# A SwiGLU / state-space / dilated-attention layer: gate output transposes as 32x32 blocks on the vector engine, and three smaller edits

## The chip, the cores and the metric

One core of one Trainium2 chip runs the whole layer. The core has five engines with a queue each: TensorE (PE in the profile, its weight loads apart as PEld), VectorE (DVE), ScalarE (ACT), GpSimd (POOL) and SyncE (SP), which here only starts DMAs. The metric is device time in microseconds of one execution, the median of several. Differences below about 0.2% can't be told from none.

## What is computed

The layer is a gated feed-forward block, a mixer (a state-space group and a dilated attention group side by side), and a second feed-forward block, each with a root-mean-square norm ahead of it; everything is float32, 256 tokens, model width 2048, hidden width 5504.

```python
def swiglu(x, w_gate, w_up, w_down):
    return (jax.nn.silu(x @ w_gate) * (x @ w_up)) @ w_down

h = h + 0.5 * swiglu(rmsnorm(h, ffn1_norm), ffn1_w_gate, ffn1_w_up, ffn1_w_down)
hn = rmsnorm(h, mix_norm)
...            # projection to q, k, v, u; s5_mixer; dilated_attention
h = h + mixed @ w_out
h = h + 0.5 * swiglu(rmsnorm(h, ffn2_norm), ffn2_w_gate, ffn2_w_up, ffn2_w_down)
return rmsnorm(h, final_norm)
```

## The kernel before

**Products in three parts.** Every large product is made of pairs of float32r halves. A weight piece of 4 x 128 rows and up to 512 columns is loaded by SP into one of three `wraw` buffers (`wraw`, L75). For two of its 128-row blocks at a time, `halves` writes the high half on ACT (L88, `whi`) and the low half on DVE (L89, `wlo`); each has four buffers. Such a pair of blocks is called a step here. `mm3` (L94 to L96) then issues three matmuls for each block and each of the two blocks of 128 tokens: high by high, high by low, low by high. A step is thus 12 matmuls. `product` (L98) walks over the steps, and between them pops work from two queues: `soon` (transposes of what has just been made) and `later` (steps of the mixer's preparation or of its scans, by `step`).

**The feed-forward block.** `ffn` (L266) goes over 11 chunks of hidden columns, ten of 512 and a last one of 384. For each it makes a gate product `G` and an up product `U` (eight steps each), then for each token block ACT writes `silu(G)` (L282) and DVE multiplies it with `U` (L283) into a tile `silu`. Its transposition is appended to `soon`: `transpose_split` (L136) makes one TensorE transpose for each 128x128 block into PSUM (L142), then ACT and DVE write the halves `xh` and `xl` of the result (L146, L147). It is popped after the second step of the next product. A full chunk has eight such transposes, the last chunk six. After the chunks, four down products `Y` over all 43 blocks use these halves, and `last_chunk` or `finish_chunk` squares the result for the next norm.

**Start and end.** `setup` issues 12 matmuls on zeros (L203) while the first pieces are loaded. In the very first gate product the input comes transposed from HBM, is split by `split_x` (L237, L238), and its first weight piece is loaded and split in three parts of 1, 1 and 2 blocks. At the end, `ffn2` issues 24 matmuls on zeros (`probe`) beside the last norm, which runs on ACT, DVE and POOL and ends with eight DMAs of the output.

**What sets the order.** Each engine works through its own queue in order. A scheduler sets that order when the program is built, by priorities and an assumed duration of each instruction, under the dependencies; buffers are reused only when the last reader is done. During the first feed-forward block the mixer's preparation (`prepare`) stands in `later` and is worked off a piece a step; it is used up ahead of the last five chunks. In the second block `later` is empty.

Of the kernel before, what the change touches and what calls it, by code (L numbers as in the profile page):

```python
# [31 lines left out]
class Layer:  # L32
# [4 lines left out]
    def __init__(self, ctx, tc, ins, out):  # L37
        self.tc, self.nc, self.t, self.out = tc, tc.nc, ins, out
        pool = lambda name, bufs, **kw: ctx.enter_context(tc.tile_pool(name=name, bufs=bufs, **kw))
        self.const = pool("const", 1)  # L40
        self.wpool = pool("weights", 2)
        self.slots = pool("slots", NSLOT)
        self.work = pool("work", 2)
        self.psum = pool("psum", 1, space=PSUM)
        self.dram = pool("scratch", 1, space=DRAM)
        self.n = 0
        self.later = deque()
        self.soon = deque()
        self.fetch = None

# [30 lines left out]

    def halves(self, raw):

        nc = self.nc
        _, nk, n = raw.shape
        hi = self.wpool.tile([P, 2, 512], F32R, tag="whi", bufs=4, name=self.name("whi"))
        lo = self.wpool.tile([P, 2, 512], F32R, tag="wlo", bufs=4, name=self.name("wlo"))
        nc.scalar.activation(hi[:, :nk, :n], raw, AF.Copy)  # L88
        nc.vector.tensor_sub(lo[:, :nk, :n], raw, hi[:, :nk, :n].bitcast(F32))  # L89
        return hi, lo  # L90
# [6 lines left out]

    def product(self, accs, xT, w, r0, nkt, c0, n, tail=0):  # L98


        held = []
        for k0 in range(0, nkt, 4):
# [3 lines left out]
            if self.fetch is not None:  # L106
                self.fetch(k0 // 4 + 1)
            xh, xl = xT[k0 // 4]
            for kk, ke in ((0, 1), (1, 2), (2, 4)) if opening else ((0, 2), (2, 4)):
# [3 lines left out]
                if self.fetch is not None:  # L113
                    self.split_x(k0 + kk, k0 + ke)
                wh, wl = self.halves(raw[:, kk:ke, :n])
                for k in range(kk, ke):
# [10 lines left out]
                while self.soon and k0 + kk >= 2:  # L127
                    self.soon.popleft()()
                self.step()
        for mm in held:  # L130
# [5 lines left out]
    def transpose_split(self, pair, src, tb, nt, gain=None):  # L136
# [11 lines left out]
        else:  # L148
            for k in range(nt):
                pk = ps[:, k * P : (k + 1) * P]  # L150
                nc.scalar.activation(hi[:, k, ts], pk, AF.Copy, scale=gain[:, k : k + 1])
                nc.vector.scalar_tensor_tensor(
                    lo[:, k, ts], pk, gain[:, k : k + 1], hi[:, k, ts].bitcast(F32),
                    op0=ALU.mult, op1=ALU.subtract,
                )

    def stat(self, nchunk):
# [30 lines left out]
    def setup(self):  # L188
# [10 lines left out]
        warm = self.slot([P, 512], F32R, s="warm")  # L199
        nc.vector.memset(warm.bitcast(F32), 0.0)  # L200
        idle = self.acc("idle")
        for _ in range(12):
            nc.tensor.matmul(idle, warm[:, :P], warm, start=True, stop=True)  # L203
# [62 lines left out]
    def ffn(self, wg, wu, wd, finish, tail=0):  # L266
        nc = self.nc
        gT = []
        for c0, n in FCH:
            G = [self.acc("g") for _ in range(NTB)]  # L270
            self.product(G, self.xT, wg, 0, 16, c0, n)
            self.xraw = None
# [6 lines left out]
            gT.append(pair)  # L279
            for tb in range(NTB):  # L280
                s = self.tmp([P, 512], "silu", 2)
                nc.scalar.activation(s[:, :n], G[tb][:, :n], AF.Silu, scale=self.r[tb])  # L282
                nc.vector.scalar_tensor_tensor(  # L283
                    s[:, :n], U[tb][:, :n], self.r[tb], s[:, :n], op0=ALU.mult, op1=ALU.mult
                )
                self.soon.append(partial(self.transpose_split, pair, s, tb, n // P))
        self.xT = [None] * 4
        self.st = self.stat(4)
        for c in range(4):
            Y = [self.acc("y") for _ in range(NTB)]  # L290
            self.product(Y, gT, wd, 0, D_FF // P, c * 512, 512, tail if c == 3 else 0)
            for tb in range(NTB):
# [633 lines left out]
    def ffn2(self):  # L926
# [3 lines left out]
        out = self.out  # L930
        self.probe()
        for tb in range(NTB):
# [13 lines left out]

    def probe(self):

        z, zb = self.idle
        mm = partial(self.nc.tensor.matmul, start=True, stop=True)  # L950
        p = [self.trp("idle") for _ in range(2)]
        for i in range(4):
            mm(p[0], z[:, :P], z)
        for i in range(4):
            mm(p[0], z[:, i * P : (i + 1) * P], z)
        for i in range(4):
            mm(p[0], zb[:, i * P : (i + 1) * P], zb[:, :512])
        for i in range(4):
            mm(p[0][:64], z[:, i * P : i * P + 64], z)
        for i in range(4):  # L960
            mm(p[i % 2], z[:, i * P : (i + 1) * P], z)
        for i in range(4):
            mm(p[0][:, :256], z[:, i * P : (i + 1) * P], z[:, :256])

    def last_chunk(self, c):
        nc = self.nc
        if c == 2:
            self.idle = self.slot([P, 512], F32R, s="z"), self.slot([P, 512], mybir.dt.bfloat16, s="zb")
            nc.gpsimd.memset(self.idle[0].bitcast(F32), 0.0)
            nc.gpsimd.memset(self.idle[1], 0.0)  # L970
        if self.gfin is None:
# [85 lines left out]
```

## Time and profile before

| what | value |
|---|---|
| median of 3 runs | 1820.44 us (1820.23 to 1821.0) |
| the profiled execution | 1820.6 us, of which the span from the first to the last instruction is 1818.7 us |
| busy in the span: PE, DVE, ACT, POOL | 1810.3, 1033.5, 862.1, 91.5 us |
| 16 DMA engines | 200 GB/s on average, between 121 and 322 GB/s by fortieth of the span |
| TensorE clock granted | 1.000 of full speed over the span |

The span and the 1.9 us outside it make the execution's time. In the views a line such as `1274.34 0.39 PE L94 MATMUL g<-whi,xh ... x1` gives the start in the span, the time from the first start to the last end of what is merged in it, the engine, the line of the kernel, the operation and its tiles (written from read). A matmul that runs in a row with others overlaps the next one, so its cost is the distance between two starts and not its own duration. In square brackets stands how long the engine had been idle, and what ended that.

### The profile page before, as it was taken

How to read it: one execution, taken by the hardware profiler on the slowest of the kernel's cores; microseconds unless marked ns; L12 is line 12 of the kernel's file. 1: busy time of each engine (PE TensorE's matmuls, PEld its weight loads, DVE VectorE, ACT ScalarE, POOL GpSimd, SP SyncE). 2: the span in 40 equal slices, each digit the busy share in tenths (PEclk: the TensorE clock that was granted, in tenths of full speed). 3: DMA queues.
4: the chain of work that ended last, by engine and by line, in shares of the span. 5: the costliest groups of instructions: out<-in, count | busy, mean ns of one | idle time of the engine just before them, and what ended most of it. 6: DMA issues, size and time to landing. Idle time of an engine off the chain costs nothing.

```text
span 1818.7 us, 21868 instructions
## 1 busy us (share of the span) xinstructions
PE 1810.3 (100%) x8514; PEld 1519.8 (84%) x8515; DVE 1033.5 (57%) x1532; ACT 862.1 (47%) x1205; POOL 91.5 (5%) x175
## 2 busy tenths in 40 slices
PE   9999999999999999999999999999999999999999
PEld 7888888888988888888888888888888888988887
DVE  5796688545445544566666565544555544544553
ACT  6544567444444444443368555444444444444443
POOL 2102022500000000000000000000000000000000
PEclk9999999999999999999999999999999999999999
DMA  8667667855555557676544455555555555755553
GB/s 322 201 213 239 206 244 248 282 186 184 187 197 190 192 189 259 214 264 242 161 139 139 139 176 191 189 185 186 192 194 191 185 186 171 224 198 183 207 191 121
DMA packets 180327, 364.16 MB, mean 200 GB/s; under 512 B 8256, under 2 KB 17344, under 8 KB 179968
## 3 DMA queue, kind: packets, MB, share of 16 engines
q1 hardware_dynamic: 172192, 343.96, 56.6%
q0 software_dynamic: 6736, 16.69, 2.7%
q10 hardware_dynamic: 1296, 2.13, 0.4%
q8 instruction: 66, 1.08, 0.2%
q14 instruction: 37, 0.30, 0.0%
HBM read 346.36 MB, written 16.38 MB: 199 GB/s over the span
## 4 chain that ended last, share of the span: by engine, by line
PE 99%; DMA 1%; SPq 0%; DVE 0%; ACT 0%; issue 0%
PE u L94 9%; PE u L96 9%; PE y L96 9%; PE u L95 9%; PE y L95 9%; PE y L94 9%; PE g L95 9%; PE g L96 9%; PE g L94 8%; PE pr L94 3%; PE pr L96 3%; PE pr L95 3%; PE tr L142 2%; PE wo L94 2%; PE wo L96 2%; PE wo L95 2%
## 5 line engine op out<-in xcount | busy, mean ns | idle before, releaser
L89 DVE TENSOR_TENSOR wlo<-wraw,whi 128x1024 fp32r<-128x1024 f32 (+2 forms) x633 | 760.3, 1203 | 715.1 <-ACT whi L88 714.2
L88 ACT ACTIVATE whi<-wraw 128x1024 fp32r<-128x1024 f32 (+2 forms) x633 | 659.1, 1043 | 845.3 <-PE y L96 258.0
L94 PE MATMUL g<-whi,xh 128*128 128x512 f32 (+1 forms) x704 | 272.6, 388 | 2.0 <-ACT xh L237 1.5
L95 PE MATMUL g<-wlo,xh 128*128 128x512 f32 (+1 forms) x704 | 270.8, 385 | 1.1 <-DVE wlo L89 1.1
L94 PE MATMUL u<-whi,xh 128*128 128x512 f32 (+1 forms) x704 | 270.7, 385 | 0.0
L96 PE MATMUL g<-whi,xl 128*128 128x512 f32 (+1 forms) x704 | 270.5, 385 | 0.0
L96 PE MATMUL u<-whi,xl 128*128 128x512 f32 (+1 forms) x704 | 270.4, 384 | 0.0
L95 PE MATMUL u<-wlo,xh 128*128 128x512 f32 (+1 forms) x704 | 270.3, 384 | 0.0
L94 PE MATMUL y<-whi,xh 128*128 128x512 f32 x688 | 268.1, 390 | 0.0
L96 PE MATMUL y<-whi,xl 128*128 128x512 f32 x688 | 267.7, 389 | 0.0
L95 PE MATMUL y<-wlo,xh 128*128 128x512 f32 x688 | 267.7, 389 | 0.0
L94 PEld LDWEIGHTS g<-whi,xh 128*128 128x128 f32 x704 | 132.0, 188 | 27.8 <-ACT xh L237 2.2
L95 PEld LDWEIGHTS g<-wlo,xh 128*128 128x128 f32 x704 | 132.2, 188 | 26.3 <-DVE wlo L89 1.9
L96 PEld LDWEIGHTS g<-whi,xl 128*128 128x128 f32 x704 | 132.1, 188 | 25.0
L95 PEld LDWEIGHTS u<-wlo,xh 128*128 128x128 f32 x704 | 132.2, 188 | 24.9
L96 PEld LDWEIGHTS u<-whi,xl 128*128 128x128 f32 x704 | 132.1, 188 | 25.0
L94 PEld LDWEIGHTS u<-whi,xh 128*128 128x128 f32 x704 | 132.1, 188 | 24.8
L95 PEld LDWEIGHTS y<-wlo,xh 128*128 128x128 f32 x688 | 129.2, 188 | 26.9
L96 PEld LDWEIGHTS y<-whi,xl 128*128 128x128 f32 x688 | 129.1, 188 | 26.7
L94 PEld LDWEIGHTS y<-whi,xh 128*128 128x128 f32 x688 | 129.1, 188 | 26.6
L94 PE MATMUL pr<-whi,xh 128*128 128x512 f32 x256 | 101.9, 398 | 0.0
L96 PE MATMUL pr<-whi,xl 128*128 128x512 f32 x256 | 100.2, 391 | 0.0
(221 smaller groups left out, 1450.1 us busy)
## 6 DMA issues: line engine op xcount, KB each, us to landing
wraw<-in_ffn_w_up SPq DMA_DIRECT2D x80, 1024.0 KB, 5.1
wraw<-in_ffn_w_down SPq DMA_DIRECT2D x80, 1024.0 KB, 5.0
wraw<-in_ffn_w_gate SPq DMA_DIRECT2D x79, 1024.0 KB, 5.1
wraw<-in_w_in SPq DMA_DIRECT2D x32, 1024.0 KB, 5.6
wraw<-in_w_out SPq DMA_DIRECT2D x16, 1024.0 KB, 5.0
wraw<-in_ffn_w_gate SPq DMA_DIRECT2D x8, 768.0 KB, 4.4
wraw<-in_ffn_w_up SPq DMA_DIRECT2D x8, 768.0 KB, 4.4
wraw<-in_ffn_w_down SPq DMA_DIRECT2D x8, 768.0 KB, 4.3
```

Source lines behind the costliest of these rows:

```text
L88: nc.scalar.activation(hi[:, :nk, :n], raw, AF.Copy)
L89: nc.vector.tensor_sub(lo[:, :nk, :n], raw, hi[:, :nk, :n].bitcast(F32))
L94: nc.tensor.matmul(out, xh, wh, start=first, stop=False)
L95: nc.tensor.matmul(out, xh, wl, start=False, stop=False)
L96: nc.tensor.matmul(out, xl, wh, start=False, stop=last)
L142: nc.tensor.transpose(ps[:, k * P : (k + 1) * P], src[:, k * P : (k + 1) * P], self.ident)
```

## The change

Four things change.

- **Transposes.** Where `later` is empty when a chunk is finished (the last five chunks of the first block and all eleven of the second), `turn_split` takes the place of `transpose_split`. For each of the two token blocks it queues 16 DVE transposes, each of one quarter of the partitions (32) by 32 columns of each 128-column block, into one SBUF tile `turned`. `product` pops up to three of them after each step, from a new queue `turns`; when the last is done, one ACT and one DVE instruction write the halves of the whole chunk. Before a product reads a pair of halves, what is left in `turns` for it is worked off. This removes 14 x 8 + 2 x 6 = 124 TensorE transposes and adds 16 x 32 = 512 DVE transposes.
- **First product.** The first gate product is built in written order (`manual_schedule`) instead of the scheduler's order.
- **Start and end.** Ten matmuls on zeros instead of 12 ahead of the first product, a small activation that loads ACT's table early, and no `probe` with its two POOL memsets.
- **Four low halves on POOL.** In the second down product of the second block, the second step of the pieces at blocks 8, 16, 24 and 32 has its low half written by POOL instead of DVE.

```diff
-    def halves(self, raw):
+    def halves(self, raw, pool=False):
...
-        nc.vector.tensor_sub(lo[:, :nk, :n], raw, hi[:, :nk, :n].bitcast(F32))
+        (nc.gpsimd if pool else nc.vector).tensor_sub(lo[:, :nk, :n], raw, hi[:, :nk, :n].bitcast(F32))
...
             if self.fetch is not None:
                 self.fetch(k0 // 4 + 1)
+            while any(x is xT[k0 // 4] for x, _ in self.turns):
+                self.turns.popleft()[1]()
             xh, xl = xT[k0 // 4]
...
-                wh, wl = self.halves(raw[:, kk:ke, :n])
+                wh, wl = self.halves(raw[:, kk:ke, :n], k0 in pooled and kk == 2)
...
                 while self.soon and k0 + kk >= 2:
                     self.soon.popleft()()
+                for _ in range(min(3, len(self.turns))):
+                    self.turns.popleft()[1]()
                 self.step()
...
+    def turn_split(self, pair, src, nt):
+        nc = self.nc
+        hi, lo = pair
+        raw = self.slot([P, 4, SEQ], s="turned")
+
+        def turn(tb, a, b):
+            nc.vector.transpose(
+                raw[32 * b : 32 * b + 32, :nt, tb * P + 32 * a : tb * P + 32 * a + 32],
+                src[tb][32 * a : 32 * a + 32, : nt * P].rearrange("p (k q c) -> p q k c", q=4, c=32)[:, b],
+            )
+
+        def split():
+            nc.scalar.activation(hi[:, :nt], raw[:, :nt], AF.Copy)
+            nc.vector.tensor_sub(lo[:, :nt], raw[:, :nt], hi[:, :nt].bitcast(F32))
+
+        for tb in range(NTB):
+            for a in range(4):
+                for b in range(4):
+                    self.turns.append((pair, partial(turn, tb, a, b)))
+        self.turns.append((pair, split))
...
+        nc.scalar.activation(self.tmp([P, 1], "rstd", 6), warm[:, :1].bitcast(F32), AF.Copy)
         idle = self.acc("idle")
-        for _ in range(12):
+        for _ in range(10):
             nc.tensor.matmul(idle, warm[:, :P], warm, start=True, stop=True)
...
-            self.product(G, self.xT, wg, 0, 16, c0, n)
+            with self.tc.manual_schedule() if self.fetch is not None else nullcontext():
+                self.product(G, self.xT, wg, 0, 16, c0, n)
...
-                self.soon.append(partial(self.transpose_split, pair, s, tb, n // P))
+            if self.later:
+                for tb, s in enumerate(src):
+                    self.soon.append(partial(self.transpose_split, pair, s, tb, n // P))
+            else:
+                self.turn_split(pair, src, n // P)
...
-            self.product(Y, gT, wd, 0, D_FF // P, c * 512, 512, tail if c == 3 else 0)
+            self.product(Y, gT, wd, 0, D_FF // P, c * 512, 512, tail if c == 3 else 0,
+                         (8, 16, 24, 32) if tail and c == 1 else ())
...
-        self.probe()
```

On PE, at the border between the first and the second chunk of the second feed-forward block, the gate product `g` of the second chunk stood like this before, with the transposes between its second and third step (`tr` is a PSUM tile, `ident` the identity):

```order
L96 MATMUL g_9211<-whi_9230,xl_8575 128x512
L142 MATMUL tr_9246<-ident,silu_9204 128x128 x4
L142 MATMUL tr_9253<-ident,silu_9207 128x128 x4
L94 MATMUL g_9210<-whi_9262,xh_8678 128x512
L95 MATMUL g_9210<-wlo_9263,xh_8678 128x512
```

With the change, at the same place:

```order
L97 MATMUL g_9322<-whi_9344,xl_8685 128x512
L95 MATMUL g_9321<-whi_9365,xh_8788 128x512
L96 MATMUL g_9321<-wlo_9366,xh_8788 128x512
L97 MATMUL g_9321<-whi_9365,xl_8789 128x512
L95 MATMUL g_9322<-whi_9365,xh_8788 128x512
```

The third step follows the second directly; elsewhere PE's row of matmuls differs in the other 15 such places, the first product, the two matmuls on zeros at the start and those of `probe`, and in nothing else.

On DVE, at the same border, from the low halves (`wlo`) of the next gate product's first three steps on, before:

```order
L89 TENSOR_TENSOR wlo_9215<-wraw_9212,whi_9214 128x1024
L89 TENSOR_TENSOR wlo_9231<-wraw_9212,whi_9230 128x1024
L89 TENSOR_TENSOR wlo_9263<-wraw_9260,whi_9262 128x1024
L283 SCALAR_TENSOR_TENSOR silu_9204<-u_9064,rstd_8892,silu_9204 128x512
L283 SCALAR_TENSOR_TENSOR silu_9207<-u_9065,rstd_8896,silu_9207 128x512
L89 TENSOR_TENSOR wlo_9279<-wraw_9260,whi_9278 128x1024
L89 TENSOR_TENSOR wlo_9297<-wraw_9294,whi_9296 128x1024
L89 TENSOR_TENSOR wlo_9313<-wraw_9294,whi_9312 128x1024
L147 TENSOR_TENSOR xl_9203<-tr_9246,xh_9202 128x4x128
L147 TENSOR_TENSOR xl_9203<-tr_9253,xh_9202 128x4x128
```

With the change, from the two products with `u` on (lows of the fourth to the eighth step):

```order
L313 SCALAR_TENSOR_TENSOR silu_9315<-u_9175,rstd_9006,silu_9315 128x512
L170 STREAM_TRANSPOSE turned_9320<-silu_9314 32x4x32 x9
L90 TENSOR_TENSOR wlo_9385<-wraw_9363,whi_9384 128x1024
L170 STREAM_TRANSPOSE turned_9320<-silu_9314 32x4x32 x3
L90 TENSOR_TENSOR wlo_9406<-wraw_9403,whi_9405 128x1024
L170 STREAM_TRANSPOSE turned_9320<-silu_9314 32x4x32 x4
L170 STREAM_TRANSPOSE turned_9320<-silu_9315 32x4x32
L90 TENSOR_TENSOR wlo_9425<-wraw_9403,whi_9424 128x1024
L170 STREAM_TRANSPOSE turned_9320<-silu_9315 32x4x32 x9
L90 TENSOR_TENSOR wlo_9446<-wraw_9443,whi_9445 128x1024
L170 STREAM_TRANSPOSE turned_9320<-silu_9315 32x4x32 x6
L90 TENSOR_TENSOR wlo_9465<-wraw_9443,whi_9464 128x1024
```

The 32 transposes stand 9, 3, 5, 9 and 6 ahead of the lows of steps four to eight. Where the next gate product is the 384-wide one, they stand 9, 3, 3, 4, 7 and 6 ahead of the lows of steps four to nine. In both, one `xl` of the whole chunk follows, then the low of the next step.

On PE, in the first product, the first step of the second weight piece, before:

```order
L94 MATMUL g_97<-whi_164,xh_107 128x512
L94 MATMUL g_98<-whi_164,xh_107 128x512
L95 MATMUL g_97<-wlo_165,xh_107 128x512
L96 MATMUL g_97<-whi_164,xl_108 128x512
L95 MATMUL g_98<-wlo_165,xh_107 128x512
```

With the change:

```order
L95 MATMUL g_97<-whi_166,xh_109 128x512
L96 MATMUL g_97<-wlo_167,xh_109 128x512
L97 MATMUL g_97<-whi_166,xl_110 128x512
L95 MATMUL g_98<-whi_166,xh_109 128x512
L96 MATMUL g_98<-wlo_167,xh_109 128x512
```

One matmul instead of two now stands ahead of the first that reads the low half.

## Rows read from the trace of the kernel before

**Rows 1.** The page: busy time by engine, and the chain by engine.

```profile
PE 1810.3 (100%) x8514; PEld 1519.8 (84%) x8515; DVE 1033.5 (57%) x1532; ACT 862.1 (47%) x1205; POOL 91.5 (5%) x175
...
PE 99%; DMA 1%; SPq 0%; DVE 0%; ACT 0%; issue 0%
```

**Rows 2.** Waits of PE, whole span: waiter, releaser, us in total, times, longest.

```profile
PE g L94 <- ACT xh L237: 1.5, 1, 1.5
...
PE g L95 <- DVE wlo L89: 1.1, 2, 0.5
```

**Rows 3.** Timeline of PE at the end of the span (columns: start, us, engine).

```profile
1814.24 0.63 PE L963 MATMUL idle<-z 128*128 128x256 f32 x4
```

**Rows 4.** Waits of SP's queue in the last 11 us.

```profile
SPq L1051 <- DMA out<-h: 3.3, 3, 1.9
```

**Rows 5.** Timeline of PE, transposes of a full chunk in the second block.

```profile
1146.52 1.04 PE L142 MATMUL tr<-ident,silu 128*128 128x128 f32 x8
...
1147.62 0.39 PE L95 MATMUL g<-wlo,xh 128*128 128x512 f32 x1
```

**Rows 6.** Timeline of PE, transposes of the last chunk in the second block.

```profile
1580.56 0.82 PE L142 MATMUL tr<-ident,silu 128*128 128x128 f32 x6
...
1581.45 0.40 PE L95 MATMUL y<-wlo,xh 128*128 128x512 f32 x1
1581.68 0.39 PE L96 MATMUL y<-whi,xl 128*128 128x512 f32 x1
```

**Rows 7.** Groups of DVE by shape: count, then busy us, mean ns, idle before.

```profile
L542 DVE TENSOR_TENSOR tt<-pow,cin 128x128 f32<-128x128 f32 x64 | 15.0, 285 | 0.0
...
L842 DVE STREAM_TRANSPOSE u<-silu 128x512 f32<-128x512 f32 x4 | 2.8, 713 | 0.9 <-ACT silu L735 0.9
...
L615 DVE TENSOR_TENSOR dm<-ident,d 32x512 f32<-32x512 f32 x2 | 1.3, 684 | 3.4 <-DMA d<-in_ssm_d 3.4
```

**Rows 8.** Timeline of all engines, border between two 512-column chunks, second block.

```profile
1274.06 1.41 DVE L283 SCALAR_TENSOR_TENSOR silu<-u,rstd,silu 128x512 f32<-128x512 f32 x2
...
1274.34 0.39 PE L94 MATMUL g<-whi,xh 128*128 128x512 f32 x1
...
1275.64 1.23 DVE L89 TENSOR_TENSOR wlo<-wraw,whi 128x1024 fp32r<-128x1024 f32 x1 [0.17 <-ACT whi L88]
...
1277.26 1.06 ACT L88 ACTIVATE whi<-wraw 128x1024 fp32r<-128x1024 f32 x1 [1.66 <-PE g L96]
...
1278.36 1.23 DVE L89 TENSOR_TENSOR wlo<-wraw,whi 128x1024 fp32r<-128x1024 f32 x1 [1.49 <-ACT whi L88]
```

**Rows 9.** The same where the 384-column gate product follows.

```profile
1540.38 1.43 DVE L283 SCALAR_TENSOR_TENSOR silu<-u,rstd,silu 128x512 f32<-128x512 f32 x2 [0.20 <-PE u L96]
...
1540.86 0.33 PE L94 MATMUL g<-whi,xh 128*128 128x384 f32 x1
...
1544.05 0.96 DVE L89 TENSOR_TENSOR wlo<-wraw,whi 128x768 fp32r<-128x768 f32 x1 [1.15 <-ACT whi L88]
...
1546.13 0.96 DVE L89 TENSOR_TENSOR wlo<-wraw,whi 128x768 fp32r<-128x768 f32 x1 [1.12 <-ACT whi L88]
```

**Rows 10.** Timeline of PE and ACT in the first 18 us.

```profile
1.46 5.46 PE L203 MATMUL idle<-warm 128*128 128x512 f32 x12 [1.46 <-DVE warm L200]
...
8.42 0.50 PE L94 MATMUL g<-whi,xh 128*128 128x512 f32 x1 [1.50 <-ACT xh L237]
...
14.70 2.01 ACT L88 ACTIVATE whi<-wraw 128x1024 fp32r<-128x1024 f32 x2 [1.01 <-DMA wraw<-in_ffn_w_gate]
...
15.81 0.73 PE L94 MATMUL g<-whi,xh 128*128 128x512 f32 x2 [0.41 <-ACT whi L88]
...
17.07 0.50 PE L95 MATMUL g<-wlo,xh 128*128 128x512 f32 x1 [0.53 <-DVE wlo L89]
```

**Rows 11.** Groups of POOL by shape.

```profile
L562 POOL MEMSET C<- 128x1024 f32 x8 | 7.8, 977 | 0.0
L171 POOL TENSOR_TENSOR rstd<-rstd,even 128x1 f32<-128x1 f32 x10 | 6.4, 644 | 626.1 <-DVE rstd L169 382.1 <-DVE rstd L170 244.0
```

More of the change, by code (lines that the diff above doesn't have):

```diff
@@ L2 @@
 from collections import deque
-from contextlib import ExitStack
+from contextlib import ExitStack, nullcontext
 from functools import partial
@@ L48, in __init__ @@
         self.soon = deque()
+        self.turns = deque()
         self.fetch = None
@@ L96, in mm3, with product @@
         nc.tensor.matmul(out, xl, wh, start=False, stop=last)
-    def product(self, accs, xT, w, r0, nkt, c0, n, tail=0):
+    def product(self, accs, xT, w, r0, nkt, c0, n, tail=0, pooled=()):
         held = []
@@ L279, in ffn @@
             gT.append(pair)
-            for tb in range(NTB):
-                s = self.tmp([P, 512], "silu", 2)
+            src = [self.tmp([P, 512], "silu", 2) for _ in range(NTB)]
+            for tb, s in enumerate(src):
                 nc.scalar.activation(s[:, :n], G[tb][:, :n], AF.Silu, scale=self.r[tb])
@@ L285, in ffn @@
                 )
-                self.soon.append(partial(self.transpose_split, pair, s, tb, n // P))
+            if self.later:
+                for tb, s in enumerate(src):
+                    self.soon.append(partial(self.transpose_split, pair, s, tb, n // P))
+            else:
+                self.turn_split(pair, src, n // P)
         self.xT = [None] * 4
@@ L945, in ffn2 @@
                 (nc.sync if c % 2 else nc.scalar).dma_start(out[tb, :, cs], hs)
[L947 to L963, printed above, removed]
     def last_chunk(self, c):
         nc = self.nc
[L967 to L970, printed above, removed]
         if self.gfin is None:
```

## The prediction

> **What bounds the kernel now.** I read the page first: PE is busy for 1810.3 of 1818.7 us, DVE for 1033.5, and the chain that ended last is PE for 99% [rows 1]. Then PE's waits over the whole span: besides the start of the zeros they are 1.5 us for the first `xh`, 1.1 us for low halves and 0.4 us for a high half, all in the first product [rows 2, 10]. After 17.07 us PE never waits again until the last product. Then the end: PE's last matmuls belong to `probe` and are over before 1815 [rows 3], while SP waits 3.3 us for output DMAs until just ahead of the end [rows 4]; so the chain's last pieces, which name `probe`, aren't what ends the span. From the first product to the last, then, the time is the sum of PE's instruction distances: an instruction taken off PE shortens it by its distance, as long as high and low halves still come early enough.
>
> **What the 124 transposes cost on PE.** In a full chunk the eight start at 1146.52, and the second matmul behind them at 1147.62 [rows 5]; without them it would start one distance after 1146.52. That distance is 0.23 us (1581.45 to 1581.68) [rows 6]. So eight cost 1.10 - 0.23 = 0.87 us, and six cost 1581.45 - 1580.56 - 0.23 = 0.66 us. Fourteen groups of eight and two of six: 14 x 0.87 + 2 x 0.66 = **13.5 us** off PE. The groups in the first block stand between the same matmuls, so one price serves.
>
> **What comes on DVE, and what hides it.** At each of 16 borders two `xl` from PSUM go, one `xl` from SBUF and 32 block transposes come. No row shows a transposition of 32 partitions by 128 columns. An operation on 32 partitions by 512 takes 684 ns, and a transposition of 128 by 512 takes 713 [rows 7], so the price goes by columns and a transposition is priced about like other operations. One of 128 columns takes 285 ns, and 64 of them were busy for 15.0 us, 0.23 us each where they overlap [rows 7]. Bounds: 0.23 us below, 0.71 above (as for 512 columns). I take c = 0.29, since the nearest row by columns is 285 and the blocks are strided.
>
> All this waits behind the two products with `u`, and the low halves of the next steps wait behind it, and PE for those. Count from the start of the next gate product, 1274.34 [rows 8]. A step is 12 x 0.227 = 2.72 us, which is the distance of the lows, 1275.64 to 1278.36. Step n needs its low (n-1) x 2.72 + 0.23 us after the start. DVE is done with the products at 1275.47, that is 1.13. Lows one to three are ahead of them. The low of step eight has all 32 transposes and five lows of 1.23 up to and with itself: 1.13 + 32c + 6.15 = 7.28 + 32c, which is 16.6 with c = 0.29, needed at 19.3. Spare: 2.7 us. The low of step nine, after the new `xl` (priced as a low, 1.23), is there at 19.0 and needed at 22.0. The earlier ones have more. The limit is c = 0.375.
>
> The narrow border is the one ahead of the 384-column gate product, once in each block. Steps there take 2.08 us (1544.05 to 1546.13) and lows 0.96; DVE is done with the products 0.95 after the start [rows 9]. The low of step nine is there at 0.95 + 32c + 6 x 0.96 = 6.71 + 32c = 16.0, needed at 8 x 2.08 + 0.17 = 16.8. The low of step ten, behind `xl`: 18.2, needed at 18.9. Spare 0.7 us; the limit is c = 0.312. So with c = 0.29 nothing is lost, and DVE's work is costed at nothing because these spares cover it. ACT has one `xh` of 1024 columns for two of 512, about the price of a high half, 1.06 us [rows 8]. It waits for the last transposition (15.3 us into a usual border), and the high half of step nine stands behind it: 15.3 + 1.06 + 1.06 = 17.5, needed at 21.8. Weight loads wait for lows, but three buffers hold six steps, and a load is started at most some 3 us later than before. In the last chunk's border the transposes are shorter and the steps 2.72 us, so there is more room. After the border DVE catches up: in a chunk of 16 steps, 43.5 us, it has 16 x 1.23 + 1.41 + 9.3 + 1.23 = 31.6 us.
>
> **The first product.** PE's first product matmul stood at 8.42 because ACT did two high halves ahead of the first `xh`; in written order it comes earlier. But the second piece's weights land at 14.70, its high half lets PE go at 15.81, and PE had by then done all it could and waited 0.41 [rows 10]. SP issues the same loads but for the order of the first two, so 14.70 stays, and what is won ahead of it is lost there. Then PE has one matmul instead of two to do before the low at 17.07: one distance is lost, **+0.23 us**. Bounds: a gain of 0.9 (both waits of 0.41 and 0.53 gone, if the loads land earlier), a loss of 3.0 (the three waits of rows 2 and 10 once more, if matmuls scattered between loads stay at the distance of those on zeros, 12 in 5.46 us, about 0.44 each). I take 0.23, which follows from the order itself. Two matmuls on zeros fewer and the earlier table load lie in PE's wait ahead of 8.42: nothing. If PE's wait were gone, they would be worth 0.9 us.
>
> **The end and POOL.** `probe` ran beside the last norm and ended 3.8 us ahead of the span: its removal is worth nothing. The four low halves on POOL have no row. POOL needs 0.98 us to write 128 x 1024, and 0.64 us for an operation of two inputs on a single column [rows 11]; DVE needs 1.23 for such a low [rows 8]. A high starts when its buffer comes free, three steps ahead of its use; so a POOL low may take 3 x 2.72 + 0.23 - 1.06 = 7.3 us before PE waits, six times DVE's time. From 0.98 to 7.3 us it costs nothing, and I take nothing.
>
> **Sum.** 13.5 - 0.23 = 13.3 us. The span of 1818.7 becomes 1805.4, the profiled execution's 1820.6 becomes 1807.3, and since that one lies 0.16 above the median of the runs shown, the median becomes **1807.1**.
>
> **Rivals.** *DVE becomes the bound at the borders.* If a block transposition costs more than about 0.4 us, the lows come late: at twelve usual borders 32(c - 0.375) each, at two narrow ones 32(c - 0.312) each. The saving is used up where 384(c - 0.375) + 64(c - 0.312) = 13.3, at c = 0.396. With c = 0.45 it is 28.8 + 8.8 - 13.3 = 24 us slower, 1844; at 0.71 it would be over 140 us. For it: the pattern (32-column blocks taken at a distance of 128, written to other partitions) has no row. Against it: the trace's transposes, which also read or write blocks at a distance, cost only 4% more than a plain operation [rows 7]. The Trainium skill, "VectorE: DVE Perf Modes", section "Rules for kernel authors", speaks for this rival: it sends whole 128x128 transposes to TensorE and only 32x32 ones to the vector engine. By engine time the trace agrees, 0.87 us on PE against 32 x 0.29 = 9.3 us on DVE for a full chunk; but here only what ends last counts. *Only the narrow borders and the opening give back.* With c = 0.33 each narrow border loses 0.6 us, and the opening up to 3.0: 1809 to 1811.5. *POOL is late.* At 12 us each the four lows cost 4 x 4.7 = 19 us, 1826; it decides from 7.3 us. The Trainium skill, "GPSIMD Engine Reference", "Elementwise — side-by-side cycle accounting", gives 1.96 times DVE's time for such an operation, by which I estimate 2.4 us and no wait; no row of this case shows it. *The saving doesn't show* because something else paces PE: against it, the loads average 200 GB/s where one stretch reached 322, and PE's chain has no wait in it, so only an overlooked dependency could do that; 1820.
>
> **How the numbers follow.** Forecast as summed 0.80; partly given back (1809 to 1811.5) 0.12; no change 0.03; slower through DVE 0.04, through POOL 0.01. The range: below, 1807.1 less the opening's possible 1.1 (0.9 and the 0.23), some transposes at 0.23 us changing nothing, and 1 us for what I read off two groups: 1805.0. Above, into the second case: 1810.5. 0.2% is 3.6 us, about what can be told from no change here: faster 0.92, same 0.03, slower 0.05.
>
> **What would show it.** Right: PE's waits still sum to some 3 us in the opening and none at the borders; at a border the matmuls of steps two and three stand 0.23 apart; block transposes of 0.23 to 0.31 us each; PE's busy time near 1791 (1810.3 less 13.5, some 5 of `probe` and 0.9 of zeros). Wrong: waits of `g` or `u` on `wlo` some 16 us into a chunk (DVE), above all in the 384-column one; waits of `y` on POOL's lows; a wait in the opening longer than those before.

## The result and the profile after

| | before | after |
|---|---|---|
| median (4 runs each) | 1820.46 us (1820.23 to 1821.0) | 1809.81 us (1808.24 to 1811.3) |
| ratio, 95% interval | | 0.9941 (0.9924 to 0.9958) |
| profiled execution, span | 1820.6, 1818.7 us | 1809.42, 1807.6 us |

The kernel became 10.65 us faster; the sum said 13.3. The median lies inside the range, but not at the forecast's 1807.1: it lies in the band of the second rival, 1809 to 1811.5. Where the missing 2.7 us went is in the trace. Busy time and chain, as in [rows 1]:

```profile
PE 1792.1 (99%) x8365; PEld 1502.2 (83%) x8365; DVE 1174.1 (65%) x2024; ACT 859.3 (48%) x1190; POOL 99.9 (6%) x177
...
PE 93%; DVE 3%; DMA 1%; issue 1%; ACT 1%; POOL 0%; SPq 0%; POOLq 0%; ACTq 0%
```

PE is still the bound, but DVE now has 3% of the chain. PE's waits on other engines' halves over the whole span (us in total, times, longest; compare [rows 2]), and then those from 300 to 1800 us alone:

```profile
PE g L96 <- DVE wlo L90: 2.6, 5, 0.8
PE g L95 <- ACT whi L89: 2.1, 2, 1.4
```

```profile
PE g L96 <- DVE wlo L90: 0.9, 2, 0.7
```

The waits of the opening sum to 3.8 us, and two waits for low halves, 0.9 us together, are new behind 300 us, both at the first border shown below; the prediction had none there. (The shortest waits don't stand in this view: those of the narrow borders are read from the timeline below.)

**A usual border** (answers [rows 8]): timeline (start, us) of DVE from the two products with `u` to the low of step eight, and of PE at the start of the gate product (1269.45), at its third step and at the next gate product.

```profile
1269.16 1.40 DVE L313 SCALAR_TENSOR_TENSOR silu<-u,rstd,silu 128x512 f32<-128x512 f32 x2
...
1269.45 0.39 PE L95 MATMUL g<-whi,xh 128*128 128x512 f32 x1
...
1270.48 2.82 DVE L170 STREAM_TRANSPOSE turned<-silu 32x128 f32<-32x128 f32 x9
...
1273.33 1.23 DVE L90 TENSOR_TENSOR wlo<-wraw,whi 128x1024 fp32r<-128x1024 f32 x1
...
1274.66 0.39 PE L97 MATMUL g<-whi,xl 128*128 128x512 f32 x1
...
1274.89 0.39 PE L95 MATMUL g<-whi,xh 128*128 128x512 f32 x1
...
1285.59 1.23 DVE L90 TENSOR_TENSOR wlo<-wraw,whi 128x1024 fp32r<-128x1024 f32 x1
...
1312.97 0.39 PE L95 MATMUL g<-whi,xh 128*128 128x512 f32 x1
```

Steps two and three stand 0.23 us apart. The low of step eight is done at 1286.82, 17.4 us after the start, needed at 19.3: 1.9 us spare (predicted 2.7). From this gate product to the next takes 1312.97 - 1269.45 = 43.52 us; before it took 44.42, from the 1274.34 of [rows 8] to this row of its timeline:

```profile
1318.76 0.39 PE L94 MATMUL g<-whi,xh 128*128 128x512 f32 x1
```

So a usual border gives 0.90.

**A narrow border** (answers [rows 9]): the 384-column gate product starts at 465.01.

```profile
479.12 1.90 DVE L170 STREAM_TRANSPOSE turned<-silu 32x128 f32<-32x128 f32 x6
...
481.05 0.96 DVE L90 TENSOR_TENSOR wlo<-wraw,whi 128x768 fp32r<-128x768 f32 x1
...
481.68 0.34 PE L95 MATMUL u<-whi,xh 128*128 128x384 f32 x1
482.07 0.44 PE L96 MATMUL u<-wlo,xh 128*128 128x384 f32 x1
```

The low of step nine is done at 482.01, 17.0 us after the start, needed at 481.85: PE's matmul starts 0.22 late, the next ones and those of the low of step ten another 0.25. This narrow border gives 0.40 instead of 0.87, the one in the second block 0.42.

**The first border with block transposes** (first block, right behind the mixer's preparation; the gate product starts at 332.93):

```profile
332.98 1.29 DVE L650 TENSOR_TENSOR dm<-ident,d 32x512 f32<-32x512 f32 x2 [2.98 <-DMA d<-in_ssm_d]
334.31 1.22 DVE L652 TENSOR_TENSOR H<-H,dm 32x1024 f32<-32x1024 f32 x1
335.56 1.23 DVE L90 TENSOR_TENSOR wlo<-wraw,whi 128x1024 fp32r<-128x1024 f32 x1
336.71 1.40 DVE L313 SCALAR_TENSOR_TENSOR silu<-u,rstd,silu 128x512 f32<-128x512 f32 x2
338.03 2.81 DVE L170 STREAM_TRANSPOSE turned<-silu 32x128 f32<-32x128 f32 x9
340.87 1.23 DVE L90 TENSOR_TENSOR wlo<-wraw,whi 128x1024 fp32r<-128x1024 f32 x1
...
342.15 0.50 PE L96 MATMUL g<-wlo,xh 128*128 128x512 f32 x1 [0.68 <-DVE wlo L90]
```

DVE idles 2.98 us for the mixer's vector `d`, so the low of step three, the products and nine turns come late, and the low of step four is done at 342.10, 9.2 us after the start; it is needed at 8.4. Over 13 steps from its start this product takes 1.5 us more than 156 x 0.2268; before it was 0.87, the price of the TensorE transposes. So this border loses 0.6 instead of gaining 0.87.

### The profile page after: what moved, and what is told of

It is laid out like the page before. It is cut to its first block, busy times and chain, and to the rows that moved or that the text cites. A ratio compares the mean times of both kernels' runs of the same rounds, so it can differ in the third digit from the quotient of the medians.

```text
span 1807.6 us, 22050 instructions
## 1 busy us (share of the span) xinstructions
PE 1792.1 (99%) x8365; PEld 1502.2 (83%) x8365; DVE 1174.1 (65%) x2024; ACT 859.3 (48%) x1190; POOL 99.9 (6%) x177
## 4 chain that ended last, share of the span: by engine, by line
PE 93%; DVE 3%; DMA 1%; issue 1%; ACT 1%; POOL 0%; SPq 0%; POOLq 0%; ACTq 0%
PE y L96 9%; PE y L95 9%; PE y L97 9%; PE u L96 8%; PE u L97 8%; PE u L95 8%; PE g L96 7%; PE g L97 7%; PE g L95 7%; PE pr L95 3%; PE pr L97 3%; PE pr L96 3%; PE wo L95 2%; PE wo L97 2%; PE wo L96 2%; DVE turned L170 1%
## 5 line engine op out<-in xcount | busy, mean ns | idle before, releaser
L90 DVE TENSOR_TENSOR wlo<-wraw,whi 128x1024 fp32r<-128x1024 f32 (+2 forms) x629 | 752.1, 1201 | 551.2 <-ACT whi L89 548.4
L170 DVE STREAM_TRANSPOSE turned<-silu 32x128 f32<-32x128 f32 (+1 forms) x512 | 152.8, 298 | 8.1
```

The lines of the kernel that those rows point to most:

```text
L90: (nc.gpsimd if pool else nc.vector).tensor_sub(lo[:, :nk, :n], raw, hi[:, :nk, :n].bitcast(F32))
L170: nc.vector.transpose(raw[32 * b : 32 * b + 32, :nt, tb * P + 32 * a : tb * P + 32 * a + 32], src[tb][32 * a : 32 * a + 32, : nt * P].rear ...
```

## The experiments

Medians are set beside the kernel before of the same chip, by their ratio; the changed kernel's own is 0.9941. Differences of a few tenths are read from the traces, matmul by matmul (the n-th matmul of the large products in one trace against the n-th in another).

**no_turns: what the other three edits are worth.**

```diff
-            if self.later:
+            if True:
                 for tb, s in enumerate(src):
                     self.soon.append(partial(self.transpose_split, pair, s, tb, n // P))
```

> The changed kernel, but with TensorE transposes at every border as before: what is left of the change is the written order of the first product, the start, the end and the four low halves on POOL. Theory (the 124 transposes carry the whole gain, the other three edits sum to +0.1 to +0.4 us): median 1820.5 to 1820.9, equal to the kernel before, with a spread under 1 us. Rival (the other edits carry a part): 1818 to 1819.5. If the opening or the end spreads the times, the spread of 3 us stays here.

Measured 1820.61 us (10 runs, 1819.79 to 1821.25), ratio 0.9996 (0.9986 to 1.0005): the transposes carry the gain, the rest is worth nothing that can be measured. The runs spread by 1.5 us here, so the edits to the start and end don't bring a spread of 3.

**old_opening and probe_kept.**

```diff
-        nc.scalar.activation(self.tmp([P, 1], "rstd", 6), warm[:, :1].bitcast(F32), AF.Copy)
         idle = self.acc("idle")
-        for _ in range(10):
+        for _ in range(12):
...
-            with self.tc.manual_schedule() if self.fetch is not None else nullcontext():
+            with nullcontext():
```

> The changed kernel, but with the opening of the kernel before: 12 matmuls on zeros, no early table load, the first product in the scheduler's order. Theory (the opening is worth between -0.2 and +0.2 us on average; how it comes out differs from run to run by up to 2.7 us in either order, with the landing of the first loads and the time at which the clock is granted): the first product matmul near 8.4 instead of 5.4 to 5.9, the 49th between 21.2 and 24, median 1809 to 1811. Rival (the written order is what makes it differ): the 49th at 22.2 as in the kernel before, and a spread under 1 us.

Measured 1810.34 us, ratio 0.9939 (0.9925 to 0.9954), four runs between 1809.19 and 1811.02. Its first product matmul starts at 9.27, its 49th at 21.96; in the kernel before at 8.42 and 22.20. In the twelve traces of the written order that these runs gave, the changed kernel's among them, the first stands at 5.3 to 5.9 and the 49th between 21.23 and 23.87 (22.26 in the changed kernel's). What is won by the earlier start is lost by the 49th, on average; a single execution may differ by 2.6 us.

```diff
         out = self.out
+        self.probe()
...
```

> The changed kernel, but with the 24 matmuls on zeros at the end (and the two POOL memsets for them) as before. Theory (removing them was worth nothing; the last output DMA decides the end): from the last product matmul to the end of the span it takes 9.2 to 9.5 us in either case; median 1809.8 within 0.5, and the spread stays as it is. Rival (the end got longer by 0.3 us and less even because PE is idle there): median 1809.5 and a spread under 1 us like the kernel before.

Measured 1810.32 us (1808.74 to 1811.31), ratio 0.9939 (0.9927 to 0.9952): the same. From the last product matmul's start to the span's end it takes 9.4 us here, 9.5 in the changed kernel, 9.1 in no_turns, which has no `probe` either: the 0.3 us by which the changed kernel's end is longer than before doesn't come from `probe`, and over all runs the end varies from 9.1 to 9.7.

**d_early: the wait for `d`.**

```diff
-        pw = self.slot([P, 2, 9, NB], s="pow")
+        pw = self.slot([P, 19, NB], s="pow")
+        self.d = d = pw[:, 18].rearrange("p (b f) -> p b f", f=2)
...
+        pw = pw[:, :18].rearrange("p (i k) b -> p i k b", i=2)
...
-        d = self.slot([P, 16, 2], s="d")
+        d = self.d
```

The four loads of `d` move with it, to the second line's place, and the step of the preparation that they made falls away.

> The changed kernel, but the mixer's vector d (32 partitions x 32 values) is loaded ahead of the preparation's group loop into spare columns of the tile that holds the powers, so that DVE need not wait for it just ahead of the first border with block transposes; its own step in the preparation falls away. Nothing else is altered. Theory (the wait for d): at that border PE now loses 1.4 us against the kernel before (two gaps of 1.07 and 0.60 us); with d early the gaps go and the median falls from 1809.8 to 1808.4. If the landing of d is also what spreads the changed kernel's times (1808.2 to 1811.3, where the kernel before spread 0.8), the spread falls under 1 us. Rival (DVE's work at that border is what is too much, not the wait: 2.5 us of the mixer's and 2.5 us of products and lows beside 10 us of turns): the gaps stay above 1 us and the median at 1809.8. Rival for the spread (the end of the kernel or the opening): it stays near 3 us.

Measured 1808.35 us (1807.86 to 1810.51), ratio 0.9932 (0.9919 to 0.9944). At the border PE now has no wait at all: the 13 steps take 156 x 0.2268 within 0.02, 1.5 us less than in the changed kernel. (The medians alone, 0.9932 against 0.9941, couldn't tell the two kernels apart.) PE's waits between 300 and 1790 us, whole list:

```profile
PE u L96 <- DVE wlo L90: 0.7, 1, 0.7
```

That one stands at 314 us, ahead of the border, and gives 1.0 back. Several other runs lose 0.2 to 0.4 us against the changed kernel at the same place, with its order, so that place is at its edge too. The theory on the border holds, but not by this run alone: here `dm` and `H` also run earlier, between 320 and 325 us, so the wait and the mixer's work left the border together. The table below parts them. The one on the spread doesn't: it stays 2.7 us, and on this chip the kernel before spread by 2.8 too. The landing of `d` is nevertheless one source. Five traces have the same order at this border and differ only in when DVE could start on `d`, counted from the gate product's start:

| kernel | `d` used at | 13 steps take longer by |
|---|---|---|
| changed kernel | 0.05 us | 1.50 us |
| pool_lows | 0.73 | 2.19 |
| probe_kept | 0.75 | 2.19 |
| old_opening | 1.08 | 2.57 |
| narrow_help | 1.60 | 4.09 (TensorE's clock fell) |

The loss is 1.45 us and the landing, one for one (the last row is below), so it is the wait: the mixer's work is the same in all five, and by this line a landing some 1.5 us ahead of the product's start would leave no loss (an estimate). With TensorE transposes the same wait is hidden for a while only: in the kernel before `d` was used at 0.49 us and nothing was lost, in no_turns at 1.24, and 0.6 us were lost. The changed kernel's profiled execution was the luckiest of these. In d_early the opening was the unlucky part: PE waited 2.80 us for a high half, and the granted clock then stood at half (the columns are busy us of PE, PEld, DVE, ACT and POOL, then PEclk, DMA share and GB/s):

```profile
8.00:10.00 2.00, 0.24 (x1) 0.19 (x1) 0.26 (x1) 0.92 (x2) 1.18 (x3) 1.00 1.05 404
10.00:12.00 2.00, 1.77 (x6) 0.86 (x5) 1.22 (x3) 1.51 (x3) 0.93 (x2) 0.92 1.05 403
12.00:14.00 2.00, 1.34 (x3) 0.79 (x3) 1.80 (x3) 1.07 (x3) 0.51 (x2) 0.50 1.04 394
14.00:16.00 2.00, 2.00 (x6) 1.54 (x5) 0.21 (x1) 0.81 (x1) 0.00 (x0) 0.50 1.05 383
```

From 14 to 16 us PE is busy throughout with matmuls 0.43 us apart; at full clock they stand 0.23 apart.

**wide: fewer, longer transposes.**

```diff
-        def turn(tb, a, b):
+        def turn(a, b):
             nc.vector.transpose(
-                raw[32 * b : 32 * b + 32, :nt, tb * P + 32 * a : tb * P + 32 * a + 32],
-                src[tb][32 * a : 32 * a + 32, : nt * P].rearrange("p (k q c) -> p q k c", q=4, c=32)[:, b],
+                raw[32 * b : 32 * b + 32, :nt].rearrange("p k (t q c) -> p q t k c", t=NTB, c=32)[:, a],
+                src[32 * a : 32 * a + 32, :, : nt * P].rearrange("p t (k q c) -> p q t k c", q=4, c=32)[:, b],
...
-        for tb in range(NTB):
-            for a in range(4):
-                for b in range(4):
-                    self.turns.append((pair, partial(turn, tb, a, b)))
+        for a in range(4):
+            for b in range(4):
+                self.turns.append((pair, partial(turn, a, b)))
...
+            both = self.tmp([P, NTB, 512], "both", 1)
...
```

> The changed kernel, but both token blocks of a gate output stand in one tile, and one block transposition takes 32 partitions by 2 x 128 columns: 16 instead of 32 at each border. From the rows 0.303 us for 128 columns and 0.713 for 512, one should take about 0.44 us, so a border's turns cost DVE 7.1 us instead of 10.05. The order puts 9, 3, 3, 1 of them ahead of the lows of steps four to seven at a usual border, and 12, 3, 1 ahead of the lows of steps five to seven where the 384-column product follows and at the first border of the first block. Theory A (what counts is how much DVE work stands ahead of one low, against that step's own need): usual borders lose nothing; a narrow border loses 2.0 us (low five done at 0.95 + 0.96 + 12 x 0.45 + 0.96 + 2.1 of waiting for its high = 10.3, needed at 8.5) where it now loses 0.5; the first border loses 1.9 where it now loses 1.4; median 1813. Theory B (DVE's work summed over a border counts): the losses of 0.5, 0.5 and most of 1.4 vanish, median 1807.5.

Measured 1808.78 us, ratio 0.9932 (0.9919 to 0.9946). One transposition takes 0.436 us (estimate 0.44), and DVE is busy 41 us less. Theory A's first half holds: at the first border the loss grew, though DVE had 3 us less to do, because 12 turns now stand ahead of one low; the 13 steps took 2.3 us longer, with a wait of 2.0 us on the low of step five:

```profile
338.81 5.37 DVE L170 STREAM_TRANSPOSE turned<-both 32x256 f32<-32x256 f32 x12
344.21 1.23 DVE L90 TENSOR_TENSOR wlo<-wraw,whi 128x1024 fp32r<-128x1024 f32 x1
```

That is 0.8 us more than in the changed kernel, but not all of it is the order's: `d` was used at 0.43 us in this trace, 0.4 later than in the changed kernel's. If the landing counts one for one here too, 0.4 us are left for the order, near the 0.5 of theory A (1.9 for 1.4).

Its second half fell by an error of mine: I added 2.1 us of waiting for a high half that was long there. Without it the narrow border's low five is due at 8.3 us and needed at 8.5. The trace has 8.3, and each narrow border gains 0.26 over the changed kernel.

**twice: DVE as the bound.**

```diff
-                    self.turns.append((pair, partial(turn, tb, a, b)))
+                    self.turns += [(pair, partial(turn, tb, a, b))] * 2
...
-                for _ in range(min(3, len(self.turns))):
+                for _ in range(min(6, len(self.turns))):
```

> The changed kernel, but every block transposition is issued twice (64 instead of 32 at a border, up to six popped after a step). Theory (DVE's due times, as in the prediction, with the measured distance of 0.314 us): a usual border has 17, 6, 6, 5, 6, 6, 6, 6 and 6 turns ahead of the lows of steps four to twelve; the low of step twelve is done at 1.13 + 64 x 0.314 + 9 x 1.23 = 32.3 us and needed at 30.15, so each of the 12 usual borders loses 2.1 us and each of the two narrow ones 6.6; the last chunk's borders lose nothing. Against the changed kernel that is 25 + 12 = 37 us more: about 1847, above the kernel before. Rival (DVE has room on average, 65% busy, and the lows' lead takes it up): 1810 to 1815.

Measured 1871.58 us, ratio 1.0276 (1.0256 to 1.0297): the prediction's rival of a slower kernel is real, and 64 turns at a border are enough for it. It is 62 us more than the changed kernel, not 37. A usual border loses 3.25, not 2.1, and each narrow one 7.2, not 6.6:

```profile
1214.90 1.23 DVE L90 TENSOR_TENSOR wlo<-wraw,whi 128x1024 fp32r<-128x1024 f32 x1
1216.16 1.92 DVE L170 STREAM_TRANSPOSE turned<-silu 32x128 f32<-32x128 f32 x6
1218.11 1.23 DVE L90 TENSOR_TENSOR wlo<-wraw,whi 128x1024 fp32r<-128x1024 f32 x1
1219.36 1.93 DVE L170 STREAM_TRANSPOSE turned<-silu 32x128 f32<-32x128 f32 x6
```

A low and six turns take 3.21 us, where I counted 1.23 + 6 x 0.314 = 3.11. Half of the difference is that the doubled turns stand 0.32 us apart instead of 0.314 (six in 1.92), the other half that each change between a low and turns costs some 0.03 (1214.90 + 1.23 to 1216.16). Over the nine lows and 64 turns that I summed this comes to about 1.0 us, most of what I had too little. The first border lost 6.4 us, the last chunk's borders 2.9 each, where I had none.

**pool_lows and narrow_help: what POOL can take.**

```diff
-                         (8, 16, 24, 32) if tail and c == 1 else ())
+                         range(0, 43, 4) if tail else ())
```

> The changed kernel, but in all four down products of the second block the second step of every piece, 44 instead of four, has its low half written by POOL. Theory (a POOL low takes 2.40 us and has 7.3 before PE waits): no wait of PE on them, DVE's lows stay at 1.23 us, time as that of the changed kernel, 1808 to 1811.5. Rival (POOL and DVE hinder each other): the lows of either grow where they overlap, PE waits on wlo in the down products, and the time grows by more than 2 us.

Measured 1809.58 us in one run. In the changed kernel (the group below: busy us, mean ns, idle before) four POOL lows take 2.40 us each; here 40 of the same width take 2.42 and four of half the width 1.29, and PE waits for none of them. DVE's lows alternate with POOL's and seldom meet them; one that began 0.90 us behind a POOL low took 2.67 us instead of 1.23, without a wait of PE. So the theory's 1.23 for all of DVE's lows isn't quite right: the rival's mechanism exists, but there is room for it here.

```profile
L90 POOL TENSOR_TENSOR wlo<-wraw,whi 128x1024 fp32r<-128x1024 f32 x4 | 9.6, 2400 | 556.2 <-ACT whi L89 556.2
```

The meeting, in pool_lows (timeline of POOL, then of DVE):

```profile
1579.58 2.49 POOL L90 TENSOR_TENSOR wlo<-wraw,whi 128x1024 fp32r<-128x1024 f32 x1 [5.03 <-ACT whi L89]
...
1580.48 2.67 DVE L90 TENSOR_TENSOR wlo<-wraw,whi 128x1024 fp32r<-128x1024 f32 x1 [0.67 <-ACT whi L89]
```

```diff
-                self.product(G, self.xT, wg, 0, 16, c0, n)
+                self.product(G, self.xT, wg, 0, 16, c0, n, 0, (8,) if n < 512 else ())
```

> The changed kernel, but in the 384-column gate products POOL, which stands idle there, writes the low half of the sixth step, so DVE has one low of 0.96 us less ahead of the low of step nine. Theory (at the narrow borders DVE is late by the last tenths: low nine is done 17.0 us after the product's start and needed at 16.8, and the 0.5 us that each of the two borders loses follow from that): both losses vanish, PE has no wait of over 0.1 us between the two narrow borders' steps; about 1 us of the whole. Rival (the loss comes from something else that stands at the change from the gate to the up product there, the weight load or the ACT's single high half of 1024 columns): 0.5 us stay at the ninth step.

One run took 1813.68 us, and the theory fell: each narrow border lost 1.1 us instead of 0.5. The timeline of POOL and DVE at the first of them:

```profile
473.17 1.84 POOL L90 TENSOR_TENSOR wlo<-wraw,whi 128x768 fp32r<-128x768 f32 x1 [115.00 <-ACT whi L89]
...
473.53 2.30 DVE L90 TENSOR_TENSOR wlo<-wraw,whi 128x768 fp32r<-128x768 f32 x1
475.85 3.79 DVE L170 STREAM_TRANSPOSE turned<-silu 32x128 f32<-32x128 f32 x12
479.67 0.96 DVE L90 TENSOR_TENSOR wlo<-wraw,whi 128x768 fp32r<-128x768 f32 x1
```

DVE's low that began 0.36 us behind POOL's took 2.30 us instead of 0.96: it ended 0.82 us after POOL's did, a little less than its own 0.96, so it stood for nearly as long as POOL worked. What was taken off DVE was lost there, and the scheduler had filled the free place with turns: 12 now stand ahead of one low. The Trainium skill, "SBUF — State Buffer", section "SBUF: two separate sides", says that a VectorE operation with two SBUF inputs and a GpSimd operation that reads SBUF share a port pair, and that whichever starts first holds it for its whole instruction; the trace agrees (2.30 against 0.96 us). Another 2.6 us of this run came from the first border, where `d` was used 1.60 us late: PE waited 2.2 us for a low, and the granted clock fell to half behind it:

```profile
342.00:344.00 2.00, 0.05 (x1) 0.05 (x1) 1.91 (x5) 0.62 (x1) 2.00 (x5) 1.00 0.41 36
344.00:346.00 2.00, 2.00 (x5) 1.62 (x6) 1.94 (x4) 0.00 (x0) 2.00 (x5) 0.53 0.54 106
346.00:348.00 2.00, 2.00 (x7) 1.53 (x7) 1.91 (x5) 0.00 (x0) 2.00 (x5) 0.62 1.03 380
```

**combined, more_from_3, more_all, combined_34: how far it goes.** All four have the wide transposes and `d` early, and

```diff
     def finish_chunk(self, c, gain):
...
-        self.soon.append(transposes)
+        if c < 3 and not self.later and gain is self.g_mix:
+            self.turn_split(pair, self.h[:, :, c * 512 : (c + 1) * 512], 4, gain[:, 4 * c : 4 * c + 4])
+        else:
+            self.soon.append(transposes)
...
```

> A version that puts together what the runs so far bear out: 16 wide block transposes at a border (as in wide), d loaded early (as in d_early, its step kept), and block transposes also for the first three of the four chunks that the first feed-forward block hands to the mixer, 24 more TensorE transposes off PE, the halves of these written with the norm's gain from the turned tile. Theory: against the changed kernel the first border gains 1.4 us, the two narrow ones 0.25 each, and the three chunks 3 x 0.9 = 2.7: ratio to the kernel before 0.9916 (1805 where the kernel before takes 1820.5). Rival (DVE is late in the down products, where the squares' inputs and the gains come on top): waits of y on wlo that take back up to 2.7, ratio 0.993.

Measured 1804.40 us (1803.73 to 1805.8), ratio 0.9910 (0.9894 to 0.9927). From 30 to 1800 us PE waits for nothing in the view of waits; against the changed kernel the first border gained 1.5 us, the narrow ones 0.25 each, the three chunks 2.7 together. The other three add block transposes where the preparation runs, by a change of the condition: in order more_from_3, more_all and combined_34.

```diff
-            if self.later:
+            if self.later and c0 < 1024:
+            if False:
+            if self.later and c0 not in (1024, 1536):
```

> The version combined, with wide block transposes also at the third to sixth border of the first feed-forward block, where the mixer's preparation runs: 32 more transposes off PE. In the changed kernel's trace DVE is busy 22.1, 31.6, 35.4 and 33.1 us in the 44 to 45 us behind these borders; 16 turns of 0.45 and the new low add 7.1 + 1.2 and take 1.3 away, so it comes to 29, 39, 42 and 40. Theory A (it fits into each chunk, so each gives 0.9 us): 3.6 us less than combined, 1801 where combined takes 1804.4, ratio 0.989. Theory B (as at the first border: preparation work that stands ahead of one low takes up its lead, though the chunk has room): two or more of the four lose 1 to 2 us each, 1803 to 1807.

> The version combined, with wide block transposes at all borders. The first two borders are followed by chunks in which DVE is busy 38.6 of 43 and 42.6 of 44 us; with 7.0 more these hold 45.6 and 49.6 us of work. Theory (a chunk that DVE can't finish in its time makes PE wait for what is over, less the lead of its buffers): PE waits for 5 to 8 us in these two chunks against 1.8 gained, so 3 to 6 us more than more_from_3. Rival (the preparation simply slips to later chunks, which have room): 1.8 us less than more_from_3.

more_from_3: 1805.16 us, ratio 0.9912 (0.9898 to 0.9927), no gain over combined. The third to sixth border gained 0.8 to 0.9 each, and in the gate products behind the fifth and the sixth 2.8 and 2.5 were lost, of which the up products won back 0.4 each: theory B. The chunks had room on average, but preparation and turns stood together ahead of single lows. more_all: 1809.39 us, ratio 0.9933 (0.9916 to 0.9949), 4.2 more than more_from_3; the second border alone lost 4.9 us, with waits of up to 3.1 and the clock at half behind them. The first, whose chunk I had counted as overfull, lost nothing and gained 0.9.

> The version combined, with wide block transposes also at the third and fourth border of the first block only. In the trace of more_from_3 these two borders gained 0.9 us each and lost nothing, while the fifth and sixth gained 0.8 and lost 2.8 and 2.5. Theory (a border pays as long as no low behind it comes late; the two chunks' own work is unchanged): 1.8 us less than combined, ratio 0.990 (1802.6 where combined takes 1804.4). Rival (the work that DVE does later because of these turns reaches the next chunks): the gain of 1.8 is given back behind the fifth border, ratio 0.991.

Measured **1802.86 us** (1802.67 to 1803.79), ratio 0.9896 (0.9879 to 0.9912), the lowest median of all, though its interval overlaps that of combined. The third and fourth border gave 1.8 us by the trace; between 311 and 316 us 0.6 of it was lost again.

## Why the prediction came out right, and where its sum was off

- *PE is the bound, and a transposition off PE is worth its distance*: right. A usual border gives 0.90 us, the sum had 0.87; no_turns shows that nothing else brought the gain.
- *c = 0.29*: mis-sized. A turn takes 0.303 us and nine take 2.81, a distance of 0.314. I took the duration of one multiplication, 0.285, and let rows of them, which overlap, stand for turns; turns take a little longer and don't overlap. The difference shows in the changed kernel: first the timeline of five multiplications of the preparation, then the group of the turns (count, busy us, mean ns, idle before):

```profile
296.17 1.09 DVE L577 TENSOR_TENSOR tt<-pow,bb 128x128 f32<-128x128 f32 x5
```

```profile
L170 DVE STREAM_TRANSPOSE turned<-silu 32x128 f32<-32x128 f32 x448 | 135.6, 303 | 7.2
```

  The five take 1.09 us, 0.20 apart. The Trainium skill, "VectorE: DVE Perf Modes", section "Two Vector instructions with no wait between them", has a rule that I didn't use: an instruction whose inputs or output start in another group of 32 partitions than the last ones did starts only when all earlier ones have finished. Successive turns write to another group each time, and the trace agrees (0.314 apart, 0.303 long); two transposes over all 128 partitions, which don't change the group, do overlap (0.71 us each, both done in 1.40). That the group is the cause is argued from that rule, though: no run changes it alone.

```profile
758.46 1.40 DVE L877 STREAM_TRANSPOSE u<-silu 128x512 f32<-128x512 f32 x2 [0.45 <-ACT silu L770]
```

- *Usual borders hide it*: right, with 1.9 us spare instead of 2.7. *Narrow borders hide it up to 0.312*: c lies just above that limit, but by the prediction's sum 0.314 would have cost less than 0.1 us, with the low of step nine done at 16.76. The trace has 17.0: the sum had put the changes between turns and lows at nothing, and most of the eleven here cost some 0.03 us. So 0.47 us were lost at this border and 0.45 at the other. It was the second rival's mechanism, at 0.12 of the chance, and two signs of being wrong that the prediction names (PE late on `wlo` some 16 us into the 384-column chunk, waits at a border) appeared in small.
- *The groups in the first block stand between the same matmuls, so one price serves*: this step failed, and it is the largest miss. At the first of these borders the mixer's `dm` and `H` and the wait for `d` stood in the same DVE queue, which I hadn't looked at there. The lows' lead hid that wait before (DVE waited 3.4 us for `d` there too, the last of [rows 7]); the turns use up the same lead. It cost 1.5 us in the profiled execution, more in other traces: there the prediction was lucky, since `d` landed earliest in this one of the five in the table.
- *The opening, +0.23*: by the 49th matmul it was +0.06, and old_opening finds no difference; but single executions in written order range from -0.97 to +1.67 there (21.23 to 23.87 against 22.20), about within its bounds of -0.9 and +3.0. *`probe` is worth nothing*: right.
- *POOL's lows cost nothing between 0.98 and 7.3 us*: right, they take 2.40, and PE waits for none, in pool_lows neither.

The sum with what was measured: 13.3 + 11 x 0.03 (0.90 for 0.87) - 1.5 (first border) - 0.9 (narrow) + 0.2 (opening) - 0.3 (end) = 11.1 us; the profiled executions differ by 11.2. The median lies 0.4 us above the profiled execution of after and moved by 10.65. Why the end takes 9.1 us in one run and 9.7 in another stays open.

## What to carry to other kernels

Work moved to an engine with room is free only if no single instruction that others wait for comes late: write down, for each low half, what stands ahead of it in its queue and when it is needed, at every place where the work lands and with all that is already queued there, loads included. Where an engine's lead hides a wait today, moving work there makes the wait visible; load early what can be loaded early. Fewer and longer instructions help, but a scheduler may put more of them ahead of the same low.

## What the runs showed of the hardware

- DVE block transposes of 32 partitions: 0.270 us for 96 columns, 0.303 for 128, 0.436 for 256, one after the other without overlap; two over 128 partitions (0.71 us each) start 0.68 apart.
- A low of 128x1024, with two SBUF inputs, takes 2.40 us on POOL, 1.23 on DVE; where a DVE low began behind one on POOL it stood until that was nearly done (2.30 us instead of 0.96 in narrow_help, 2.67 instead of 1.23 in pool_lows).
- TensorE's granted clock fell to half (1.2 GHz) behind waits of 2.8 us (d_early, opening) and 2.2 us (narrow_help, first border), and cost 2.0 us (ten matmuls, 0.2 each) and 1.0 us (4.09 - 1.45 - 1.60) on top; not every such wait did it: behind one of 2.3 us in the opening of more_all the clock stayed at 1.00. A late half can cost more than its own wait.
